# SwiGLU pairs on one Trainium2 core: eleven more pairs by seven products, two kinds of PSUM tile, another order at the seams, the last two output tiles in halves

## The chip, the core and the metric

The kernel runs on one NeuronCore of a Trainium2 chip. The metric is the device time of one execution in microseconds (us). TensorE does the matmuls, VectorE and ScalarE the elementwise work, SyncE issues most of the loads; each engine has its own instruction stream, and semaphores tie them together. Matmul results land in PSUM, everything else is in SBUF.

## What is computed

Two models of depth 2 run one after the other, each on 512 tokens of width 1024. The stages at issue are the four SwiGLU layers of the second model, where 16 learned tokens stand ahead of the 512 (T = 528; the last layer drops them, T = 512):

```python
def swiglu(x, w_gate, w_up, w_down):
    return (jax.nn.silu(x @ w_gate) * (x @ w_up)) @ w_down

for l in range(DEPTH):
    h = h + 0.5 * swiglu(rmsnorm(h, norm_gains[l, 0]), ...)
    h = h + mixer(rmsnorm(h, norm_gains[l, 1]), ...)
    h = h + 0.5 * swiglu(rmsnorm(h, norm_gains[l, 2]), ...)
return rmsnorm(h, final_norm)[:, N_META:]
```

The width D_FF is 2816, so w_gate and w_up have 22 column tiles of 128 each, and w_down has 22 row tiles. All is float32.

## The kernel before, in words

**Products in three parts.** Each float32 operand is split into a high part in the type fp32r and the rest. For weights the high part, whi, is written by ScalarE (L226) and the rest, wlo, by VectorE (L227); activations are split in the same way by `split` (L235, L236). A product is then three matmuls: high by high, low by high, high by low (L241).

**Stages.** `ffn2(l, f)` is one SwiGLU layer; (0,0), (0,1), (1,0) and (1,1) name the four. Between (0,0) and (0,1), and between (1,0) and (1,1), stands a mixer; (1,0) follows (0,1) at once. A seam is the passage from the end of one such stage to the first round of the next.

**Rounds and pairs.** In ffn2 the 22 gate and up tiles of the same column form 22 pairs. They are computed in three rounds, pairs 0 to 7, 8 to 15 and 16 to 21 (`ROUNDS`); behind each round comes its down product, eight output tiles (dn) whose results are scaled (fd) and added to the residual (xt). Two kinds of pair exist. A direct pair (`whole`) is two groups of 48 matmuls at T = 528 (24 of 512 columns at T = 512), one for the gate, one for the up tile. A seven-product pair (`strassen`) gets the same from seven products p1, p2, p6, p5, p7, p4, p3 of 12 matmuls each, of half the width (264 or 256 columns). For that it needs sums of weights (`sum`, four a pair, VectorE L1049) and sums of activations, the forms: `form(k)` makes fu and fv for one of four row tiles k by one ScalarE operation, four short VectorE ones (tu, tv) and two splits (ful, fvl on VectorE). `DIRECT` names the pairs that are direct, its first tuple for (0,1), (1,0) and (1,1), its second for (0,0).

**The sums of a seven-product pair.** p1 makes Y in PSUM, and ScalarE copies it (L1104); p6, p7 and p4 go on adding to Y, each behind a copy of the stand before it. p2 makes X, p5 makes Z, to which p3 adds; VectorE adds X and Z to the copies (L1098). PSUM has three tiles of two banks (kind P) and two tiles of one bank (kind S). Before, Y and Z lie in P and X in S, and a gate or up group takes a P tile.

**The order.** Inside the rounds the order of TensorE's products is computed by `product_order`, which starts a product as soon as its operands are there by its own cost numbers, at most two pairs at a time, and TensorE is held to it. Weight loads and splits run six products ahead (`LEAD`); there are six raw, four sum and eight whi and wlo buffers. On the other engines instructions run in the order in which they stand, and a waiting one holds up those behind it.

**The seams.** Pairs 0 and 1 are direct and run ahead of the first round (`ahead`; in (0,0) pairs 0, 1 and 2, from products made earlier). Their gate and up groups g0, u0, g1 and u1 follow the arrival of the normalized input. `finish`, called for each output tile at the end of the stage before, splits the input and makes a form for k = 4, 5 and 6; the fourth form is made in the `ahead` loop, before pair 0's result is scaled (`mul_r`, L447), multiplied and split (`act`: L1207 on ScalarE, L1208 on VectorE, then fah on ScalarE and fal on VectorE).

**The end.** In (1,1) the last of the eight output tiles is computed in halves of 256 tokens by `ending`: the first half is finished (sum of squares ssq, reciprocal root by ten small VectorE steps, broadcast bc, eight final multiplications L1310 and their stores) before the second.

The change touches `DIRECT`, `finish` (L331), `strassen` (L1089), `product_order` (L1136), the `ahead` loop in `ffn2` and `ending` (L1281). The changed file has one line more near its top, so a line of before stands there a little lower: L227 becomes L228, L447 L448, L1104 L1106, L1207 L1212.

Of the kernel before, what the change touches and what calls it, by code (L numbers as in the profile page):

```python
# [22 lines left out]
NX = 512  # L23
# [30 lines left out]
DIRECT = (0, 1, 5, 12, 18), (3, 12, 18)  # L54
# [7 lines left out]
class Net:  # L62
    def __init__(self, ctx, tc, d):
        nc = self.nc = tc.nc
        self.tc = tc
        self.d = d
        self.n = 0
        self.xp = ctx.enter_context(tc.tile_pool(name="xp", bufs=1))
        self.cp = ctx.enter_context(tc.tile_pool(name="cp", bufs=1))
        self.sp = ctx.enter_context(tc.tile_pool(name="sp", bufs=NSLOT))  # L70
        self.mp = ctx.enter_context(tc.tile_pool(name="mp", bufs=24))
        self.qp = ctx.enter_context(tc.tile_pool(name="qp", bufs=8))
        self.wstack = ctx.enter_context(ExitStack())
# [257 lines left out]
    def finish(self, k, T, g):  # L331
# [4 lines left out]
        if self.forms is not None and NK // 2 <= k < NK - 1:  # L336
# [734 lines left out]
    def whole(self, i, xs, T, rb, act):  # L1071
# [3 lines left out]
        def one(o):  # L1075
            def go(w):
# [12 lines left out]
    def strassen(self, i, xs, T, rb, act):  # L1089
# [16 lines left out]
        def p2(w):  # L1106
            X = self.S("x")[:, :h]
# [3 lines left out]
        def p6(w):  # L1111
# [3 lines left out]
        def p5(w):  # L1115
            Z = ps["Z"] = self.P("z")[:, 0, :h]
            self.prod(Z, w[0], f1, a, True)

        def p7(w):
# [4 lines left out]
        def p4(w):  # L1124
# [3 lines left out]
        def p3(w):  # L1128
# [7 lines left out]
    def product_order(kinds):  # L1136


        LAT = 24
        need = {"p6": ("p1",), "p5": ("p1",), "p7": ("p6", "p5"), "p4": ("p7",), "p3": ("p7",), "p2": ("p1",)}  # L1140
        takes, frees = {"p1", "p5", "g", "u"}, {"p4", "p3", "g", "u"}
        left = [(m, o) for m, kd in enumerate(kinds) for o in (("p1", "p2", "p6", "p5", "p7", "p4", "p3") if kd == "7" else ("g", "u"))]
        end, out, t = {}, [], 0
        hold = []
        while left:
            first = left[0][0]
            best = None
            for m, o in left:
                if m > first + 1:
                    break  # L1150
                at = max([t] + [end[m, d] + (0 if (d, o) in (("p1", "p2"), ("p1", "p5"), ("p5", "p7")) else LAT) for d in need.get(o, ()) if (m, d) in end])
                if any((m, d) not in end for d in need.get(o, ())):
                    continue
                if o in takes:
                    busy = [f for f in hold if f is None or f > t]
                    if len(busy) >= 3:
                        if None in busy and sum(f is None for f in busy) >= 3:
                            continue
                        at = max(at, sorted(f for f in busy if f is not None)[len(busy) - 3])
                if best is None or at < best[0]:  # L1160
                    best = (at, m, o)
            at, m, o = best
# [3 lines left out]
            if o in takes:  # L1166
                hold = [f for f in hold if f is None or f > at]
                hold.append(t + LAT if o in ("g", "u") else None)
            elif o in frees:
                hold.remove(None)  # L1170
                hold.append(t + LAT)
            out.append((m, o))
        return out

    def ffn2(self, l, f, xs, g, next_g, out=None):
# [45 lines left out]
        for m1 in ROUNDS:  # L1221
# [24 lines left out]
            for n in range(len(order) + LEAD):  # L1246
                if n < len(order):
                    i, o = order[n]
# [3 lines left out]
                if n >= LEAD:  # L1252
                    i, o = order[n - LEAD]
# [4 lines left out]
                    do[i][o](w.pop((i, o)))  # L1258
# [16 lines left out]
            if fin and out is not None:  # L1275
                self.ending(out, self.wload(dsrc(NK - 1)), acts, rb)
# [4 lines left out]
    def ending(self, out, ws, acts, rf):  # L1281

        nc = self.nc
        ps = [self.outs(1, NX, "dn")[0][0] for _ in range(2)]
        m = NK - 1
        for hf in range(2):
            c = slice(256 * hf, 256 * hf + 256)
            bl = (2 * hf, 2 * hf + 1)
            n = len(acts)
            for k in range(n):  # L1290
                self.mm3(ps[hf], ws, 128 * k, acts[k], NX, k == 0, k == n - 1, halves=(hf,))
            xv = self.xt[m][:, c]
            t = self.slot("fd")
            nc.vector.scalar_tensor_tensor(
                out=t[:, c], in0=ps[hf][:, c], scalar=0.5, in1=rf[:, c], op0=ALU.mult, op1=ALU.mult
            )
            nc.vector.tensor_tensor(out=xv, in0=t[:, c], in1=xv, op=ALU.add)
            self.sumsq(m, xv, c)
# [4 lines left out]
            self.finals(out, bc, c)  # L1303
# [758 lines left out]
```

## Time and profile before

| what | value |
|---|---|
| median of 3 runs | 3576.71 us (3575.93 to 3577.52) |
| profiled execution, its own time | 3577.7 us |
| its span | 3575.9 us |
| granted TensorE clock, mean | 0.991 of full |
| TensorE busy | 3501.3 us |
| VectorE busy | 2437.5 us |
| ScalarE busy | 1718.5 us |

The span runs from the first to the last instruction; the profiled execution's own time holds 1.8 us more. Busy times of different engines overlap. The granted clock is what the chip gave TensorE: 1.00 stands for 2.4 GHz, 0.50 for 1.2 GHz.

### The profile page before, as it was taken

How to read it: one execution, taken by the hardware profiler on the slowest of the kernel's cores; microseconds unless marked ns; L12 is line 12 of the kernel's file. 1: busy time of each engine (PE TensorE's matmuls, PEld its weight loads, DVE VectorE, ACT ScalarE, POOL GpSimd, SP SyncE). 2: the span in 40 equal slices, each digit the busy share in tenths (PEclk: the TensorE clock that was granted, in tenths of full speed). 3: DMA queues.
4: the chain of work that ended last, by engine and by line, in shares of the span. 5: the costliest groups of instructions: out<-in, count | busy, mean ns of one | idle time of the engine just before them, and what ended most of it. 6: DMA issues, size and time to landing. Idle time of an engine off the chain costs nothing.

```text
span 3575.9 us, 59662 instructions
## 1 busy us (share of the span) xinstructions
PE 3501.3 (98%) x23291; PEld 3123.4 (87%) x23291; DVE 2437.5 (68%) x4715; ACT 1718.5 (48%) x3151; POOL 44.3 (1%) x184
## 2 busy tenths in 40 slices
PE   8999999999999999999999999999999999999998
PEld 6778888778888899998898999998999987788987
DVE  6778753776874387676545777678677764677767
ACT  3654432365543364354574454454444457545443
POOL 1000000000000000000000000000000000000000
PEclk9999999999999999999999999999999999999999
DMA  4213323212333232331111222332333212223232
GB/s 151 65 48 109 97 89 107 81 60 67 99 95 93 70 105 89 95 107 61 55 61 57 83 92 92 94 102 77 96 107 93 76 54 64 65 85 105 92 104 71
DMA packets 142954, 304.94 MB, mean 85 GB/s; under 512 B 16436, under 2 KB 24660, under 8 KB 142672
## 3 DMA queue, kind: packets, MB, share of 16 engines
q1 hardware_dynamic: 138672, 292.88, 26.1%
q0 software_dynamic: 2560, 6.93, 0.6%
q8 instruction: 183, 3.00, 0.3%
q10 hardware_dynamic: 1440, 1.32, 0.1%
q14 instruction: 99, 0.81, 0.1%
HBM read 298.97 MB, written 2.10 MB: 84 GB/s over the span
## 4 chain that ended last, share of the span: by engine, by line
PE 73%; DVE 5%; ACT 2%; issue 1%; DMA 0%; DVEq 0%; ACTq 0%
PE dn L241 15%; PE g L241 12%; PE y L241 11%; PE up L241 7%; PE gu L241 6%; PE z L241 5%; PE wo L241 3%; PE x L241 3%; PE pa L241 1%; PE pb L241 1%; PE oa L1531 1%; PE sc L1497 1%; DVE wlo L227 1%; PE go L1761 1%; PE ptr L1514 1%
## 5 line engine op out<-in xcount | busy, mean ns | idle before, releaser
L226 ACT ACTIVATE whi<-raw 128x512 fp32r<-128x512 f32 (+3 forms) x880 | 620.0, 708 | 879.2 <-PE dn L241 340.5
L227 DVE TENSOR_TENSOR wlo<-raw,whi 128x512 fp32r<-128x512 f32 (+3 forms) x880 | 687.8, 783 | 401.2 <-ACT whi L226 386.9
L241 PE MATMUL g<-xh,whi 128*128 128x256 f32 (+4 forms) x1192 | 330.4, 333 | 10.0 <-ACT xh L315 5.7
L241 PE MATMUL g<-xl,whi 128*128 128x256 f32 (+4 forms) x1192 | 317.9, 320 | 0.1
L241 PE MATMUL g<-xh,wlo 128*128 128x256 f32 (+4 forms) x1192 | 316.1, 320 | 0.0
L241 PE MATMUL up<-xl,whi 128*128 128x512 f32 (+1 forms) x768 | 288.7, 376 | 0.1
L241 PE MATMUL up<-xh,wlo 128*128 128x512 f32 (+1 forms) x768 | 288.6, 376 | 0.0
L241 PE MATMUL up<-xh,whi 128*128 128x512 f32 (+1 forms) x768 | 287.9, 376 | 0.0
L241 PE MATMUL dn<-fah,whi 128*128 128x256 f32 (+1 forms) x1238 | 286.4, 300 | 1.2 <-ACT fah L235 0.6
L241 PE MATMUL dn<-fah,wlo 128*128 128x256 f32 (+1 forms) x1238 | 285.3, 299 | 0.0
L241 PE MATMUL dn<-fal,whi 128*128 128x256 f32 (+1 forms) x1238 | 285.1, 299 | 0.0
L226 ACT ACTIVATE whi<-sum 128x512 fp32r<-128x512 f32 x268 | 169.2, 632 | 219.0 <-PE dn L241 72.4
L241 PEld LDWEIGHTS g<-xh,whi 128*128 128x128 f32 (+1 forms) x1192 | 198.0, 188 | 46.1 <-issue 18.1
L227 DVE TENSOR_TENSOR wlo<-sum,whi 128x512 fp32r<-128x512 f32 x268 | 184.2, 687 | 47.9 <-ACT whi L226 43.7
L241 PEld LDWEIGHTS g<-xh,wlo 128*128 128x128 f32 (+1 forms) x1192 | 200.3, 188 | 15.4
L241 PEld LDWEIGHTS g<-xl,whi 128*128 128x128 f32 (+1 forms) x1192 | 200.7, 189 | 14.1 <-issue 1.6
L241 PEld LDWEIGHTS dn<-fah,whi 128*128 128x128 f32 x1238 | 199.8, 188 | 10.8 <-ACT fah L235 3.9
L241 PEld LDWEIGHTS dn<-fal,whi 128*128 128x128 f32 x1238 | 199.4, 188 | 7.9 <-DVE fal L236 0.8
L241 PEld LDWEIGHTS dn<-fah,wlo 128*128 128x128 f32 x1238 | 199.7, 188 | 7.3
L241 PEld LDWEIGHTS up<-xl,whi 128*128 128x128 f32 x768 | 145.1, 189 | 28.3 <-DVE xl L316 0.5
L241 PEld LDWEIGHTS up<-xh,wlo 128*128 128x128 f32 x768 | 145.2, 189 | 28.0
L241 PEld LDWEIGHTS up<-xh,whi 128*128 128x128 f32 x768 | 144.7, 189 | 27.5
(503 smaller groups left out, 8704.0 us busy)
## 6 DMA issues: line engine op xcount, KB each, us to landing
raw<-w_up SPq DMA_DIRECT2D x88, 512.0 KB, 3.6
raw<-ffn_g SPq DMA_DIRECT2D x176, 256.0 KB, 2.6
raw<-ffn_u SPq DMA_DIRECT2D x176, 256.0 KB, 2.9
raw<-ffn_d SPq DMA_DIRECT2D x160, 256.0 KB, 2.7
raw<-w_in SPq DMA_DIRECT2D x136, 256.0 KB, 2.6
raw<-w_down SPq DMA_DIRECT2D x32, 512.0 KB, 3.5
raw<-w_in SPq DMA_DIRECT2D x25, 512.0 KB, 3.6
raw<-w_out SPq DMA_DIRECT2D x16, 512.0 KB, 3.5
```

The lines of the kernel that those rows point to most:

```text
L226: h = self.nc.scalar.activation(hi[:, c], raw[:, c], AF.Copy)
L227: l = self.nc.vector.tensor_tensor(out=lo[:, c], in0=raw[:, c], in1=hi[:, c], op=ALU.subtract)
L241: i = self.nc.tensor.matmul(*a, **k)
L1497: nc.tensor.matmul(o, lhsT=q, rhs=kk[:, kc], start=i == 0, stop=i == len(ops) - 1)
L1514: nc.tensor.transpose(tr[:, 128 * b : 128 * b + 128], p[:, 128 * b : 128 * b + 128], self.ident)
L1531: nc.tensor.matmul(o[a], lhsT=lh, rhs=rh, start=b == 0, stop=b == 4)
L1761: nc.tensor.matmul(o(b), lhsT=lh, rhs=rh, start=i == 0, stop=i == len(terms) - 1)
```

## The change

Four things are done together.

1. `DIRECT` loses pairs 5, 12 and 18 in (0,1), (1,0) and (1,1), and 12 and 18 in (0,0): by the tuples eleven direct pairs fewer, eight of them at T = 528.
2. `product_order` keeps a model of both kinds of PSUM tile and returns a kind with each product that opens one; `strassen` takes the tile from that kind. p1 prefers P, p2 and p5 prefer S.
3. At the end of the first ffn2 `early` falls from 3 to 2 and stays there, so that `finish` makes two forms ahead of each later seam. In the `ahead` loop pair 0's scaling, and in these three stages its activation too, now stand ahead of the call that makes forms.
4. `ending` works on the last two output tiles: the first half of both, their sum of squares, then the second half of both, the last of these in an S tile (dl). The broadcast is copied to SBUF by ScalarE, and all sixteen final multiplications stand behind the second reciprocal root.

```diff
-DIRECT = (0, 1, 5, 12, 18), (3, 12, 18)
+DIRECT = (0, 1), (3,)
...
+        self.early = 3
...
-        if self.forms is not None and NK // 2 <= k < NK - 1:
+        if self.forms is not None and NK // 2 <= k < NK // 2 + self.early:
             self.form(k - NK // 2, T, g)
...
+        bank = lambda kd, n: self.P(n)[:, 0, :h] if kd == "P" else self.S(n)[:, :h]
...
-        def p1(w):
-            Y = ps["Y"] = self.P("y")[:, 0, :h]
+        def p1(w, kd):
+            Y = ps["Y"] = bank(kd, "y")
...
-            X = self.S("x")[:, :h]
+            X = bank(kd, "x")
...
-            Z = ps["Z"] = self.P("z")[:, 0, :h]
+            Z = ps["Z"] = bank(kd, "z")
...
-        takes, frees = {"p1", "p5", "g", "u"}, {"p4", "p3", "g", "u"}
+        takes = {"p1": "PS", "p5": "SP", "p2": "SP", "g": "P", "u": "P"}
+        frees = {"p4": "p1", "p3": "p5", "p2": "p2", "g": "g", "u": "u"}
...
+        pool, has = {"P": [0] * 3, "S": [0] * 2}, {}
...
+                    at, _, kd = min((max(at, min(pool[q])), j, q) for j, q in enumerate(takes[o]))
...
+                gt = ps[0] if o == 4 else self.mul_r(ps[0], rb, "fg")
+                if not done:
+                    act(o // 2, gt, ps[1], False)
                 forms(1 + (o == 0) - (o == 4))
-                gt = ps[0] if o == 4 else self.mul_r(ps[0], rb, "fg")
-                act(o // 2, gt, ps[1], False)
+                if done:
+                    act(o // 2, gt, ps[1], False)
...
-                self.forms = self.next_forms
+                self.forms, self.early = self.next_forms, 2
...
-            for i in range(NK - 1 if fin and out is not None else NK):
+            for i in range(NK - 2 if fin and out is not None else NK):
...
-                self.ending(out, self.wload(dsrc(NK - 1)), acts, rb)
+                self.ending(out, [self.wload(dsrc(i)) for i in (NK - 2, NK - 1)], acts, rb)
...
-        ps = [self.outs(1, NX, "dn")[0][0] for _ in range(2)]
+        ps = [[self.outs(1, NX, "dn")[0][0] for _ in ws], [self.outs(1, NX, "dn")[0][0], self.S("dl")]]
...
-            self.finals(out, bc, c)
+            rb = self.slot("rbe")
+            nc.scalar.copy(rb[:, c], bc[:, c])
+            bcs.append((rb, c))
+        for rb, c in bcs:
+            self.finals(out, rb, c)
```

What the tables and the code order do to the engines' streams is shown at three places. VectorE at the seam of (0,1), before. Here fal closes pair 0, the row L447 scales pair 1's gate, L1208 multiplies it; ful and fvl are the fourth form's low parts, L1049 the sums of weights:

```order
L236 TENSOR_TENSOR ful_20693<-tu_20685,fuh_20692 128x528
L236 TENSOR_TENSOR fvl_20697<-tv_20686,fvh_20696 128x528
L447 TENSOR_TENSOR fg_20700<-gu_20469,rbc_20620 128x528
L227 TENSOR_TENSOR wlo_20800<-sum_20801,whi_20799 128x512
L227 TENSOR_TENSOR wlo_20806<-raw_20807,whi_20805 128x512
L1208 TENSOR_TENSOR fg_20700<-fg_20700,gu_20470 128x528
L227 TENSOR_TENSOR wlo_20812<-raw_20813,whi_20811 128x512
L236 TENSOR_TENSOR fal_20705<-fg_20700,fah_20704 128x528
L447 TENSOR_TENSOR fg_20769<-gu_20471,rbc_20620 128x528
```

VectorE at the same place, changed; between pair 0's fal and pair 1's scaling (L448) stand twenty rows, four of wlo, four of sum, eight short ones (tu, tv) and four of ful and fvl, of which these are the last eleven:

```order
L228 TENSOR_TENSOR wlo_20917<-raw_20827,whi_20916 128x512
L349 SCALAR_TENSOR_TENSOR tu_20727<-xt_79,v_74,tt_20726 128x264
L1050 TENSOR_TENSOR sum_21033<-raw_20847,sum_20881 128x512
L349 SCALAR_TENSOR_TENSOR tv_20728<-xt_83,v_74,tu_20727 128x264
L355 TENSOR_TENSOR tu_20727<-tv_20728,tt_20726 128x264
L349 SCALAR_TENSOR_TENSOR tv_20728<-xt_83,v_74,tv_20728 128x264
L237 TENSOR_TENSOR ful_20735<-tu_20727,fuh_20734 128x528
L1050 TENSOR_TENSOR sum_21056<-raw_21052,raw_21054 128x512
L237 TENSOR_TENSOR fvl_20739<-tv_20728,fvh_20738 128x528
L448 TENSOR_TENSOR fg_20803<-gu_20489,rbc_20638 128x528
L228 TENSOR_TENSOR wlo_20934<-sum_20935,whi_20933 128x512
```

Pair 0's scaling has moved ahead of the fourth form, and the third and fourth forms have moved between pair 0 and pair 1.

ScalarE at the seam of (0,1), before; L1207 is pair 1's silu, fah its split, COPY the copy of p1's Y:

```order
L226 ACTIVATE whi_20817<-sum_20819 128x512
L1207 ACTIVATE fg_20769<-fg_20769 128x528
L226 ACTIVATE whi_20839<-sum_20847 128x512
L235 ACTIVATE fah_20773<-fg_20769 128x528
L226 ACTIVATE whi_20865<-raw_20793 128x512
L1104 COPY fg_20823<-y_20825 128x264
```

And changed:

```order
L227 ACTIVATE whi_20916<-raw_20827 128x512
L352 ACTIVATE tt_20726<-xt_79,v_74 128x264
L236 ACTIVATE fuh_20734<-tu_20727 128x528
L236 ACTIVATE fvh_20738<-tv_20728 128x528
L227 ACTIVATE whi_20933<-sum_20935 128x512
L1212 ACTIVATE fg_20803<-fg_20803 128x528
L236 ACTIVATE fah_20807<-fg_20803 128x528
L1106 COPY fg_20857<-y_20859 128x264
```

The copy of p1 stands behind pair 1's silu and split as before, and these now stand behind the fourth form's splits.

TensorE at the end of the program, before; ssq is the sum of squares, bc the broadcast, dn_37976 the second half of the last tile:

```order
L241 MATMUL dn_37976<-fal_37702,whi_37970 128x256
L241 MATMUL dn_37976<-fah_37701,wlo_37971 128x256
L365 MATMUL ssq_38001<-cst,acc_37739 128x1 x2
L418 MATMUL bc_38004<-cst,rs_y_38007 128x128 x2
L365 MATMUL ssq_38069<-cst,acc_37739 128x1 x2
L418 MATMUL bc_38072<-cst,rs_y_38075 128x128 x2
```

And changed:

```order
L242 MATMUL dn_38283<-fah_38032,whi_38264 128x256
L366 MATMUL ssq_38333<-cst,acc_38070 128x1 x2
L242 MATMUL dn_38283<-fal_38033,whi_38264 128x256
L242 MATMUL dn_38283<-fah_38032,wlo_38265 128x256
L419 MATMUL bc_38336<-cst,rs_y_38339 128x128 x2
L242 MATMUL dl_38284<-fah_37421,whi_38270 128x256
```

All of the last tile's second half (dl, 18 matmuls) now follows the first broadcast.

## Rows read from the trace of the kernel before

**Rows 1.** The page, part 1: busy us, share of the span, instructions of each engine.

```profile
PE 3501.3 (98%) x23291; PEld 3123.4 (87%) x23291; DVE 2437.5 (68%) x4715; ACT 1718.5 (48%) x3151; POOL 44.3 (1%) x184
```

**Rows 2.** Windows with no other filter: four seven-product pairs of stage (0,1); window, length, busy.

```profile
2188.80:2226.90 38.10, 38.10 (x316) 38.10 (x315) 32.64 (x56) 23.10 (x46) 0.00 (x0) 1.00 0.38 121
```

**Rows 3.** PE timeline of stage (0,1), T=528: start us, us, engine, line, operation, tiles.

```profile
2103.56 0.40 PE L241 MATMUL gu<-xh,whi 128*128 128x256 f32 x2
...
2109.37 0.28 PE L241 MATMUL y<-fuh,whi 128*128 128x264 f32 x1
...
2119.55 0.29 PE L241 MATMUL y<-xh,whi 128*128 128x264 f32 x1
...
2121.01 0.28 PE L241 MATMUL x<-xh,whi 128*128 128x264 f32 x1
```

**Rows 4.** PE timeline of stage (1,1), T=512: a direct group, and the product after it.

```profile
3254.58 0.39 PE L241 MATMUL gu<-xh,whi 128*128 128x512 f32 x1
...
3260.12 0.28 PE L241 MATMUL y<-fuh,whi 128*128 128x256 f32 x1
```

**Rows 5.** Lines by form, DVE, 2180 to 2280 us: count, busy us, mean ns, idle before.

```profile
L227 DVE TENSOR_TENSOR wlo<-sum,whi 128x512 fp32r<-128x512 f32 x26 | 17.9, 688 | 5.0 <-ACT whi L226 4.5
```

**Rows 6.** PE timeline: first and last of three waits of p6 (y); idle before in brackets.

```profile
2125.23 0.39 PE L241 MATMUL y<-fvh,whi 128*128 128x264 f32 x1 [1.14 <-ACT fg L1104]
...
3275.57 0.39 PE L241 MATMUL y<-fvh,whi 128*128 128x256 f32 x1 [1.23 <-ACT fg L1104]
```

**Rows 7.** DVE timeline at the seam of (0,1): fal, pair 1's scaling, its product.

```profile
2074.70 0.71 DVE L236 TENSOR_TENSOR fal<-fg,fah 128x528 fp32r<-128x528 f32 x1
2075.32 0.70 DVE L447 TENSOR_TENSOR fg<-gu,rbc 128x528 f32<-128x528 f32 x1
...
2077.99 0.70 DVE L1208 TENSOR_TENSOR fg<-fg,gu 128x528 f32<-128x528 f32 x1
```

**Rows 8.** ACT timeline at the seam of (0,1): the copy of p1.

```profile
2079.79 0.36 ACT L1104 COPY fg<-y 128x264 f32<-128x264 f32 x1
```

**Rows 9.** PE timeline at the seam of (0,1): first matmuls of p5 (z) and p6 (y).

```profile
2080.17 0.28 PE L241 MATMUL z<-fuh,whi 128*128 128x264 f32 x1
...
2081.62 0.28 PE L241 MATMUL y<-fvh,whi 128*128 128x264 f32 x1
```

**Rows 10.** DVE timeline at the seam of (1,0): a form's short step, the next row.

```profile
2439.91 0.48 DVE L348 SCALAR_TENSOR_TENSOR tu<-xt,v,tt 128x264 f32<-128x264 f32 x1
2440.34 0.69 DVE L227 TENSOR_TENSOR wlo<-sum,whi 128x512 fp32r<-128x512 f32 x1
```

**Rows 11.** Timeline at the seam of (1,1): DVE, ACT and PE, the same places.

```profile
3228.11 0.68 DVE L447 TENSOR_TENSOR fg<-gu,rbc 128x512 f32<-128x512 f32 x1
...
3231.61 0.35 ACT L1104 COPY fg<-y 128x256 f32<-128x256 f32 x1
...
3231.86 0.28 PE L241 MATMUL z<-fuh,whi 128*128 128x256 f32 x1
...
3233.27 0.28 PE L241 MATMUL y<-fvh,whi 128*128 128x256 f32 x1
```

**Rows 12.** PE timeline at the seam of (1,0): u1's first matmul, the next product.

```profile
2445.99 0.78 PE L241 MATMUL gu<-xh,whi 128*128 128x256 f32 x2 [4.37 <-DVE fg L447]
...
2454.10 0.28 PE L241 MATMUL y<-xh,whi 128*128 128x264 f32 x1
```

**Rows 13.** Windows, seam of (1,0), columns as in Rows 2; PEclk: granted clock.

```profile
2441.60:2446.00 4.40, 0.03 (x2) 0.04 (x1) 4.40 (x9) 1.79 (x4) 0.00 (x0) 0.77 0.00 0
2446.00:2448.00 2.00, 2.00 (x9) 2.00 (x10) 1.18 (x3) 1.16 (x2) 0.00 (x0) 0.50 0.19 52
```

**Rows 14.** The chain of waits that ended last, from 3555 us: start us, us, what.

```profile
3556.95 0.62 PE ssq L365 x4
...
3560.34 3.22 DVE fy L1310 x8
...
3568.51 1.21 PE bc L418 x4
```

More of the change, by code (lines that the diff above doesn't have):

```diff
@@ L1075, in one, with go @@
         def one(o):
-            def go(w):
+            def go(w, kd):
                 p = self.outs(1, T, "gu")[0]
@@ L1122, in p7, with p4, p3 @@
             tt(u[:, b], ps["Z"], u[:, b], ALU.add)
-        def p4(w):
+        def p4(w, kd):
             self.prod(ps["Y"], w[0], f2, b, False)
             nc.scalar.copy(u[:, a], ps["Y"])
-        def p3(w):
+        def p3(w, kd):
             self.prod(ps["Z"], w[0], x2, b, False)
@@ L1140, in product_order @@
         need = {"p6": ("p1",), "p5": ("p1",), "p7": ("p6", "p5"), "p4": ("p7",), "p3": ("p7",), "p2": ("p1",)}
-        takes, frees = {"p1", "p5", "g", "u"}, {"p4", "p3", "g", "u"}
+        takes = {"p1": "PS", "p5": "SP", "p2": "SP", "g": "P", "u": "P"}
+        frees = {"p4": "p1", "p3": "p5", "p2": "p2", "g": "g", "u": "u"}
         left = [(m, o) for m, kd in enumerate(kinds) for o in (("p1", "p2", "p6", "p5", "p7", "p4", "p3") if kd == "7" else ("g", "u"))]
         end, out, t = {}, [], 0
-        hold = []
+        pool, has = {"P": [0] * 3, "S": [0] * 2}, {}
+        inf = 10**9
         while left:
@@ L1150, in product_order @@
                     break
-                at = max([t] + [end[m, d] + (0 if (d, o) in (("p1", "p2"), ("p1", "p5"), ("p5", "p7")) else LAT) for d in need.get(o, ()) if (m, d) in end])
                 if any((m, d) not in end for d in need.get(o, ())):
                     continue
+                at = max([t] + [end[m, d] + (0 if (d, o) in (("p1", "p2"), ("p1", "p5"), ("p5", "p7")) else LAT) for d in need.get(o, ())])
+                kd = None
                 if o in takes:
[L1155 to L1159, printed above, removed]
+                    at, _, kd = min((max(at, min(pool[q])), j, q) for j, q in enumerate(takes[o]))
+                    if at >= inf:
+                        continue
                 if best is None or at < best[0]:
-                    best = (at, m, o)
-            at, m, o = best
+                    best = (at, m, o, kd)
+            at, m, o, kd = best
             t = at + (48 if o in ("g", "u") else 12)
@@ L1165, in product_order @@
             left.remove((m, o))
[L1166 to L1172, printed above, removed]
+            if kd:
+                j = pool[kd].index(min(pool[kd]))
+                pool[kd][j] = inf
+                has[m, o] = kd, j
+            if o in frees:
+                q, j = has[m, frees[o]]
+                pool[q][j] = t + LAT
+            out.append((m, o, kd))
         return out
@@ L1247, in ffn2 @@
                 if n < len(order):
-                    i, o = order[n]
+                    i, o, _ = order[n]
                     if i not in get:
@@ L1252, in ffn2 @@
                 if n >= LEAD:
-                    i, o = order[n - LEAD]
+                    i, o, kd = order[n - LEAD]
                     m = ms[i]
@@ L1257, in ffn2 @@
                         do[i] = f(m - m0, xs, T, rb, act)
-                    do[i][o](w.pop((i, o)))
+                    do[i][o](w.pop((i, o)), kd)
             self.pinned = False
@@ L1283, in ending @@
         nc = self.nc
-        ps = [self.outs(1, NX, "dn")[0][0] for _ in range(2)]
-        m = NK - 1
+        ps = [[self.outs(1, NX, "dn")[0][0] for _ in ws], [self.outs(1, NX, "dn")[0][0], self.S("dl")]]
+        n = len(acts)
+        bcs = []
         for hf in range(2):
@@ L1288, in ending @@
             bl = (2 * hf, 2 * hf + 1)
[L1289 to L1298, printed above, removed]
+            for m, p, w in zip((NK - 2, NK - 1), ps[hf], ws):
+                for k in range(n):
+                    self.mm3(p, w, 128 * k, acts[k], NX, k == 0, k == n - 1, halves=(hf,))
+                xv = self.xt[m][:, c]
+                t = self.slot("fd")
+                nc.vector.scalar_tensor_tensor(
+                    out=t[:, c], in0=p[:, c], scalar=0.5, in1=rf[:, c], op0=ALU.mult, op1=ALU.mult
+                )
+                nc.vector.tensor_tensor(out=xv, in0=t[:, c], in1=xv, op=ALU.add)
+                self.sumsq(m, xv, c)
             pss = self.S("ssq")
```

8 lines of the change are left out of this document (4 added, 4 removed).

## The prediction

> **What bounds the kernel now.** The page's first part comes first: TensorE is busy for 98% of the span, VectorE for 68%, ScalarE for 48% [rows 1]. So the time is TensorE's time, and an edit pays by taking matmuls out, or costs by making TensorE stand. The share of 68% is a mean over stages, so the windows come second: in four seven-product pairs of stage (0,1) TensorE has no gap in 38.10 us, and VectorE works 32.64 us of them, 86% [rows 2]. Third, the timelines of TensorE, VectorE and ScalarE at the places that the change touches: the first round of each stage, the seams between stages, and the end.
>
> **The pairs.** By the two tuples the change turns eleven direct pairs into seven-product pairs (its words say ten): eight at T=528 and three at T=512. At T=528 one group of 48 matmuls takes 2109.37 - 2103.56 = 5.81 us, so a direct pair 11.62; one product takes 2121.01 - 2119.55 = 1.46, so seven take 10.22 [rows 3]. That saves 1.40 us, times eight 11.2. At T=512 a group takes 3260.12 - 3254.58 = 5.54 [rows 4], a pair 11.08; a product 3233.27 - 3231.86 = 1.41 [rows 11], seven 9.87; that saves 1.21, times three 3.6. Together **-14.8 us**, all of it on the path. Each new pair also asks for more of VectorE: three more weight subtractions and four weight sums, some 0.69 us each [rows 5], and three additions. That is costed at nothing: the four pairs in a row of [rows 2] are made of such pairs alone, and VectorE still has 14% to spare. If that cover were gone, the saving would go with it (a rival below). DMA issues do not grow.
>
> **Waits that go.** In the first round of (0,1), (1,0) and (1,1), p6 of the pair that follows a direct pair stands 1.1 to 1.2 us for ScalarE's copy of p1, which is queued behind the direct pair's activation [rows 6] (the first and the last of the three; the middle one took 1.13). No direct pair stands there any more, so these go: 1.14 + 1.13 + 1.23 = **-3.5 us**. In (0,0) a direct pair stays in front, and I take nothing.
>
> **PSUM kinds.** In the new order p2 and p5 take the one-bank kind S, p1 the two-bank kind P. In [rows 2] TensorE does not wait for a P tile, so a third free P tile earns nothing: 0. The cost side is a rival.
>
> **The seams of (0,1) and (1,1).** This is the term that decides. Two of the four operand forms, not one, are now left for the seam, and VectorE's order puts both behind pair 0's last subtraction (fal) and ahead of pair 1's scaling. Before, the scaling followed that fal at once, 2074.70 to 2075.32 [rows 7]. Now twenty rows stand between: four weight subtractions, four weight sums and four splits at the 0.62 us step of [rows 7], and eight short steps of forms at 2440.34 - 2439.91 = 0.43 [rows 10]. That is 12 x 0.62 + 8 x 0.43 = 10.9 us: the scaling comes at 2086.2. Two things wait. p5 needs the fourth form's first half, ready some 1.2 us before that, at 2085.0, where it began at 2080.17 [rows 9]. And p6 needs the copy of p1, which in ScalarE's order stands behind pair 1's activation and split, so behind that scaling: from scaling to copy it took 2079.79 - 2075.32 = 4.47 us [rows 7, 8]; one row fewer stands on VectorE between scaling and product now, so 3.85, and 0.36 for the copy itself. p6 then starts at 2090.4 instead of 2081.62 [rows 9]: **+8.8 us**. In (1,1) the same rows have a step of 0.60, the short ones 0.41 (estimates by the sizes, 512 to 528): 10.5 us later, scaling at 3238.6; copy 3231.61 - 3228.11 = 3.50 later, 0.35 long; p6 at 3242.5 instead of 3233.27 [rows 11]: **+9.2 us**.
>
> **The clock after them.** At the seam of (1,0) TensorE stood 4.37 us [rows 12], and in the window after it the granted clock was 0.50, the lower of the two levels (1.2 against 2.4 GHz) [rows 13]. The group that followed took 2454.10 - 2445.99 = 8.11 us instead of 5.81 [rows 12, 3]: 2.3 more. The new stalls are longer, 5 and 4 us with one product between, so each gets that price: **+4.6 us**, between 0 (the clock holds) and 4.6. The Trainium skill, "TensorE: Matmul & The Clock Gate", Part 1, says that an idle TensorE is throttled to half rate and must work for a while before it is let up again; [rows 13] agree, and by the page's rule alone the sum would hold the same 4.6.
>
> **The seam of (1,0).** Here the fourth form stood ahead of pair 0's scaling and held the 4.37 us wait. With the scaling first, that wait goes (up to 4.37 + 2.3 = 6.7 gained). But VectorE works without a break there, 4.40 us of 4.40 [rows 13], and the same rows still have to pass before p6: the wait moves from u1 to p5 and p6. I take **0**, since the row shows VectorE as the bound; ends -6.7 and +2.3 (a second half-clock stretch).
>
> **The end.** Two tiles in halves: the first sum of squares can start one half-tile group earlier (18 matmuls at half of 5.54/24 us, 2.1) and no longer behind a whole tile's addition (an estimate: 0.5): -2.6. The first eight finals, 3.22 us [rows 14], move from the middle to the end: 0, but they hide the second broadcast there (-1.2 [rows 14]). The last half tile's 18 matmuls now come behind the first broadcast: +2.1, or 4.2 at half clock. **-1.7 us**, ends -2.6 and +0.4.
>
> **Sum.** -14.8 - 3.5 - 1.7 + 8.8 + 9.2 + 4.6 + 0 = +2.6 us. The profiled execution took 3577.7 us, 1.0 above the median of the runs shown; against the median 3576.7 the sum gives **3579.3 us**: no difference that a measurement here tells (0.2% is 7.2 us, about what it can tell).
>
> **Rivals.**
> *Short seams (faster).* Only the moved third form comes on top (4 x 0.43 + 2 x 0.62 = 3.0 us a seam), because the weight rows among the twenty run in the time in which VectorE would wait anyway, and the clock holds. Then 8.8 + 9.2 + 4.6 = 22.6 becomes about 6: 3563. For it: over the whole span VectorE is idle for a third of the time [rows 1]. Against it: none of the rows of VectorE at this place shows an idle time ahead of it [rows 7]. Chance 0.17.
> *Longer seams (slower).* The weight subtractions among the twenty need buffers that only TensorE frees, and TensorE stands. Each of the two seams then loses some 3 to 4 us more: five or six more of the 0.62 us steps [rows 7], 3579.3 + 6 to 9 = 3585 to 3588. It decides when a subtraction of the twenty waits over 1 us for TensorE. Chance 0.13.
> *S as the bound (slower).* X and Z share two tiles; p2 or p5 waits until VectorE has added the Z before it. It decides once that addition comes later than two products, 2.9 us, after its product. At 0.2 us a pair and 78 pairs it costs 15.6: 3595. [rows 2] speak against it: VectorE keeps up. Chance 0.08.
> *VectorE as the bound (slower), or the pairs bring nothing.* With no direct pair to catch up in, the missing 14% is used up and the 14.8 is not earned: 3594. Against it: [rows 2]. Chance 0.05.
> *The clock in the rounds (slower).* TensorE halves in every round because tiles are handed over more often: twelve rounds at 2.3 us, 3607. The granted clock of [rows 2] is 1.00. Chance 0.02. The Trainium skill, "TensorE: Matmul & The Clock Gate", "A second HAM failure mode: psum-queue depth-cycling", tells of a kernel that cycles its PSUM banks and whose clock swings with the short idles between; no row here shows that.
> That leaves 0.55 for the forecast, whose own range is 3574 to 3585.
>
> **Numbers.** Range 3567 to 3589: it leaves out the lower half of the short seams and the last three rivals, about 0.2. Faster by over 0.2% (below 3569.6): 0.16, the short seams almost whole. Slower (above 3583.9): the three last rivals 0.15, most of the longer seams and the top of the forecast's range, 0.26 together. Within: 0.58.
>
> **What would show it.** Right: TensorE gaps of 4 to 5 us in front of p5 and p6 at 2080 to 2090 and around 3240 on the shifted scale, released by VectorE's ful and ScalarE's copy, clock 0.50 behind them; no gaps before p6 in the first rounds; a round of eight sevens without gaps; 78 copies of p1. Wrong: seams below 4 us in all, a wait of p2 on the addition of Z, or VectorE over 97% in the rounds.

## The result: slower, by waits in every round

The changed kernel takes 3598.2 us (median of 4 runs, 3596.8 to 3600.4), the kernel before beside it 3577.05 us; the ratio is 1.0060, 95% interval 1.0045 to 1.0074. Forecast were 3579.3 us and a range of 3567 to 3589: the time is above the range. Its profiled execution took 3598.57 us, span 3596.8 us, against 3577.7 and 3575.9.

The page of the changed kernel, its first line, the busy times (part 1) and one of the costliest groups (part 5; behind the second bar the idle time of TensorE just before the group, and what ended most of it):

```profile
span 3596.8 us, 59926 instructions
PE 3495.2 (97%) x23321; PEld 3121.7 (87%) x23321; DVE 2481.3 (69%) x4828; ACT 1749.1 (49%) x3231; POOL 44.4 (1%) x184
L242 PE MATMUL y<-fvh,whi 128*128 128x264 f32 (+1 forms) x624 | 181.9, 291 | 29.7 <-ACT fu L1123 18.0
```

TensorE is busy for 6.1 us less than before [rows 1], where 14.8 was worked out for the pairs, and its idle time grew from 74.6 to 101.6 us, so the span grew by 20.9 us: TensorE stands more. The third line tells where. The matmuls y<-fvh belong to p6 and p4; before them stand 29.7 us of idle time, and 18.0 of these end with ScalarE's copy L1123, that of p7. Most of the rest, 11.5 us, are waits of p6 at the seams for the copy of p1. Before, the same group by shape, T = 528, had 3.4 us of idle time in all, put down to the copy of p1 [rows 6], and none to that of p7:

```profile
L241 PE MATMUL y<-fvh,whi 128*128 128x264 f32 x400 | 115.1, 288 | 3.4 <-ACT fg L1104 3.4
```

The windows of the second round of (0,1), before, then changed, whole, and of the 9.3 us behind its longest wait, columns as in [rows 2]:

```profile
2188.80:2273.50 84.70, 84.68 (x695) 84.31 (x694) 70.14 (x117) 49.15 (x95) 0.00 (x0) 1.00 0.36 113
2196.30:2284.40 88.10, 85.72 (x688) 85.15 (x687) 73.75 (x127) 51.48 (x102) 0.00 (x0) 0.98 0.34 108
2218.70:2228.00 9.30, 9.29 (x64) 9.29 (x65) 6.70 (x13) 4.55 (x10) 0.00 (x0) 0.82 0.35 114
```

This round took 84.7 us before, with no gap. TensorE was to gain 1.4 us in it; it has no matmul for 2.4 us, and the mean granted clock of the whole round is 0.98, since it falls to 0.82 behind the wait. VectorE works 73.75 of 88.10 us, 84%: it is not at its limit.

What makes the wait, in that round. VectorE's timeline, then ScalarE's, then TensorE's:

```profile
2215.17 0.68 DVE L228 TENSOR_TENSOR wlo<-sum,whi 128x512 fp32r<-128x512 f32 x1
2215.88 0.69 DVE L1050 TENSOR_TENSOR sum<-raw,sum 128x512 f32<-128x512 f32 x1
2216.49 0.70 DVE L1213 TENSOR_TENSOR fg<-fg,fu 128x528 f32<-128x528 f32 x1
```

```profile
2217.23 0.64 ACT L236 ACTIVATE fah<-fg 128x528 fp32r<-128x528 f32 x1 [0.78 <-DVE fg L1213]
2217.78 0.61 ACT L227 ACTIVATE whi<-sum 128x512 fp32r<-128x512 f32 x1
2218.30 0.36 ACT L1123 COPY fu<-y 128x264 f32<-128x264 f32 x1
```

```profile
2218.71 0.39 PE L242 MATMUL y<-fvh,whi 128*128 128x264 f32 x1 [1.76 <-ACT fu L1123]
```

Product p7 of the second pair began at 2212.40 and takes 1.46 us, so it had ended by 2213.9, and ScalarE needs 0.36 us for the copy, yet the copy starts at 2218.30. ScalarE takes its instructions in order, and ahead of the copy stand the split of the first pair's activation (fah), which waits for VectorE's product L1213 at 2216.49, and a weight split. That product in turn stands on VectorE behind a weight subtraction and a weight sum. p4, the product that adds to the copied Y, starts 0.4 us behind the copy, 1.76 us late. Such a wait of p4 stands once in each of the twelve rounds, 1.25 to 1.76 us long, 16.9 us together, and twice a second one, 0.50 and 0.62: the 18.0 us of the page.

Why there. In the old order the second pair begins p1 p2 p6, then come the first pair's p4 and p3, then the second pair's p5 and p7. Z had to wait for a P tile. In the new order Z takes an S tile, so p5 goes ahead of the first pair's p4 and p3, and the first pair's activation comes one product, 1.46 us, later against the second pair's p7 and p4. Between the end of the first pair's p3 and the second pair's p4 TensorE then has three products to do, 4.4 us, and no longer four, while the activation and the copy queued behind it took 6.3 us from the end of p3. One product was about all the slack there was.

The seam of (0,1), changed, to be read beside [rows 7 to 9]: VectorE, ScalarE, TensorE, and the windows with the granted clock in the third column from the right:

```profile
2072.57 0.71 DVE L237 TENSOR_TENSOR fal<-fg,fah 128x528 fp32r<-128x528 f32 x1
...
2082.27 0.71 DVE L237 TENSOR_TENSOR ful<-tu,fuh 128x528 fp32r<-128x528 f32 x1 [0.30 <-ACT fuh L236]
...
2084.12 0.70 DVE L448 TENSOR_TENSOR fg<-gu,rbc 128x528 f32<-128x528 f32 x1
```

```profile
2086.79 0.64 ACT L236 ACTIVATE fah<-fg 128x528 fp32r<-128x528 f32 x1 [1.30 <-DVE fg L1213]
2087.34 0.36 ACT L1106 COPY fg<-y 128x264 f32<-128x264 f32 x1
```

```profile
2082.29 0.39 PE L242 MATMUL z<-fuh,whi 128*128 128x264 f32 x1 [2.96 <-ACT fuh L236]
...
2087.75 0.59 PE L242 MATMUL y<-fvh,whi 128*128 128x264 f32 x1 [4.09 <-ACT fg L1106]
```

```profile
2084.00:2088.00 4.00, 0.25 (x1) 0.25 (x2) 3.26 (x6) 1.72 (x4) 0.00 (x0) 0.50 0.00 0
2088.00:2090.00 2.00, 2.00 (x10) 2.00 (x11) 0.51 (x2) 0.00 (x0) 0.00 (x0) 0.50 0.00 0
```

Pair 1's scaling comes 11.55 us behind fal, where the prediction had 0.62 + 10.9; the copy of p1 3.2 us behind it. p6 waits for that copy as described; p5's first matmul is released by ScalarE's fuh, and ful holds it back by 0.35 us more. The first matmul of p1, before, then changed:

```profile
2077.24 0.28 PE L241 MATMUL y<-xh,whi 128*128 128x264 f32 x1
```

```profile
2075.15 0.28 PE L242 MATMUL y<-xh,whi 128*128 128x264 f32 x1
```

From it to the first matmul of p6 it is 2087.75 - 2075.15 = 12.60 us, and was 2081.62 - 2077.24 = 4.38 [rows 9]: +8.2. In (1,1) it is 12.62 and was 4.28: +8.3. Behind the stalls p6 and the two products after it took 7.1 and 6.1 us instead of 4.4 and 4.3, the clock's part: +4.5 in the two seams.

The end, in the chain of waits (start, duration, what), beside [rows 14]:

```profile
3575.80 0.62 PE ssq L366 x4
3578.43 1.22 PE bc L419 x4
3579.66 3.12 PE dl L242 x18
3587.22 1.98 DVE fy L1324 x5
```

The 18 matmuls of dl take 3.12 us, with a mean granted clock of 0.67 in that stretch. From the first matmul of the last two tiles to the end of the span it was 27.9 us before and is 27.5 now.

### The profile page after: what moved, and what is told of

Same layout as the page of the kernel before. It is cut to its first block, busy times and chain, and to the rows that moved or that the text cites. A ratio compares the mean times of both kernels' runs of the same rounds, so it can differ in the third digit from the quotient of the medians.

```text
span 3596.8 us, 59926 instructions
## 1 busy us (share of the span) xinstructions
PE 3495.2 (97%) x23321; PEld 3121.7 (87%) x23321; DVE 2481.3 (69%) x4828; ACT 1749.1 (49%) x3231; POOL 44.4 (1%) x184
## 3 DMA queue, kind: packets, MB, share of 16 engines
q10 hardware_dynamic: 1440, 1.32, 0.1%
## 5 line engine op out<-in xcount | busy, mean ns | idle before, releaser
L228 DVE TENSOR_TENSOR wlo<-raw,whi 128x512 fp32r<-128x512 f32 (+3 forms) x869 | 680.0, 784 | 388.3 <-ACT whi L227 376.3
L227 ACT ACTIVATE whi<-sum 128x512 fp32r<-128x512 f32 x312 | 197.0, 631 | 237.3 <-PE y L242 83.5
L228 DVE TENSOR_TENSOR wlo<-sum,whi 128x512 fp32r<-128x512 f32 x312 | 213.7, 686 | 65.5 <-ACT whi L227 63.0
L242 PE MATMUL y<-fvh,whi 128*128 128x264 f32 (+1 forms) x624 | 181.9, 291 | 29.7 <-ACT fu L1123 18.0
L242 PE MATMUL y<-fvh,wlo 128*128 128x264 f32 (+1 forms) x624 | 179.2, 287 | 0.0
L242 PE MATMUL y<-fvl,whi 128*128 128x264 f32 (+1 forms) x624 | 179.0, 287 | 0.0
```

The source lines that it names most:

```text
L227: h = self.nc.scalar.activation(hi[:, c], raw[:, c], AF.Copy)
L228: l = self.nc.vector.tensor_tensor(out=lo[:, c], in0=raw[:, c], in1=hi[:, c], op=ALU.subtract)
L242: i = self.nc.tensor.matmul(*a, **k)
```

## The experiments

Two theories stood against each other after the first reading. By *order*, the new order of products brings p4 one product nearer to the activation behind which its copy is queued, and costs that in every round whatever VectorE has to do. By *load*, VectorE is late because eleven pairs more are formed by products.

**Old order in the changed kernel.** `product_order` and the kinds of tile are those of before, all else is as changed:

```diff
-        takes = {"p1": "PS", "p5": "SP", "p2": "SP", "g": "P", "u": "P"}
-        frees = {"p4": "p1", "p3": "p5", "p2": "p2", "g": "g", "u": "u"}
+        takes, frees = {"p1", "p5", "g", "u"}, {"p4", "p3", "g", "u"}
...
+            out.append((m, o, {"p1": "P", "p5": "P", "p2": "S"}.get(o)))
```

> The changed kernel with the product order and the PSUM kinds of before (Y and Z in P, X in S); pairs, seams and ending as changed. Theory 'order': the new order brings p5 of the second pair ahead of the first pair's p4 and p3, so the first pair's activation comes one product (1.46 us) later, ScalarE's copy of the second pair's p7 (L1123) stands behind that activation's split, and the second pair's p4 waits 1.3 to 1.8 us, once in every round. With the old order these 12 waits go, with the half-clock stretches behind the longer ones: 18 to 24 us less than the changed kernel's 3598, so 3574 to 3580, and no gap over 0.5 us in the second and third rounds. Rival 'load': the waits come from VectorE, which has more weight rows to do with eleven direct pairs fewer; they stay whatever the order, 3595 to 3600.

Measured: 3574.97 us (10 runs, 3573.2 to 3576.7), 23.2 less than the changed kernel; ratio to before 0.9995 (0.9985 to 1.0004). The second round of (0,1) in its windows, and the y<-fvh groups by shape:

```profile
2189.40:2273.70 84.30, 83.90 (x687) 83.55 (x687) 73.77 (x127) 51.52 (x102) 0.00 (x0) 1.00 0.36 113
```

```profile
L242 PE MATMUL y<-fvh,whi 128*128 128x264 f32 x464 | 134.3, 290 | 2.1 <-ACT fu L1123 2.0
L242 PE MATMUL y<-fvh,whi 128*128 128x256 f32 x160 | 46.0, 288 | 0.4 <-ACT fu L1123 0.4
```

VectorE's work in the round is the same to 0.02 us, 73.77, and the waits have shrunk from 18.0 to 2.4 us. So the load alone does not make them; it takes the order. One wait of 1.34 us is left in the second round of (0,0), where no gap over 0.5 was expected. The waits are 15.6 of the 23.2 us; the rest was not taken apart. Order and kinds were changed back together, but no wait for an S tile shows in the changed kernel either: the idle time in front of p2's first matmuls (x<-xh) is 0.0. ScalarE and TensorE at the place of the wait, with the old order:

```profile
2208.03 0.65 ACT L236 ACTIVATE fah<-fg 128x528 fp32r<-128x528 f32 x1 [0.35 <-DVE fg L1210]
2208.58 0.61 ACT L227 ACTIVATE whi<-raw 128x512 fp32r<-128x512 f32 x1
2209.10 0.36 ACT L1123 COPY fu<-y 128x264 f32<-128x264 f32 x1
```

```profile
2209.83 0.28 PE L242 MATMUL y<-fvh,whi 128*128 128x264 f32 x1
```

The copy stands behind fah here too. It ends 0.4 us ahead of p4, which now comes four products behind the first pair's p3 and waits for nothing. The seam of (0,1) has one wait instead of two, in front of p5:

```profile
2081.09 0.56 PE L242 MATMUL z<-fuh,whi 128*128 128x264 f32 x1 [7.13 <-DVE fg L448]
```

Z then has to have the P tile that pair 1's scaling frees, so all of the stall stands there.

**Old seams in the changed kernel.**

```diff
+                forms(1 + (o == 0) - (o == 4))
                 gt = ps[0] if o == 4 else self.mul_r(ps[0], rb, "fg")
-                if not done:
-                    act(o // 2, gt, ps[1], False)
-                forms(1 + (o == 0) - (o == 4))
-                if done:
-                    act(o // 2, gt, ps[1], False)
+                act(o // 2, gt, ps[1], False)
...
-                self.forms, self.early = self.next_forms, 2
+                self.forms, self.early = self.next_forms, 3
```

> The changed kernel with the seams of before (three forms made by finish, forms ahead of pair 0's scaling); pairs, order and ending as changed. Theory 'order': seams and rounds add up; the two seams gave 8 to 9 us each and some 2.5 us of half clock, so this is 19 to 22 us faster than the changed kernel, 3576 to 3579, and the waits of p4 in the rounds stay as they are. Rival 'seam taken up later': the work on VectorE is the same, and what does not wait at the seam waits in the first round; under 8 us faster, over 3590.

Measured: 3583.57 us (10 runs, 3579.2 to 3589.0), 14.6 less than the changed kernel, where 19 to 22 were expected: a miss, between the two theories. The stalls of (0,1) and (1,1) are gone, that of u1 at the seam of (1,0), 4.38 us, is back, and part is taken up in the same round: the first wait of p4 in (0,1), 1.26 us in the changed kernel, is now

```profile
2103.21 0.39 PE L242 MATMUL y<-fvh,whi 128*128 128x264 f32 x1 [2.35 <-ACT fu L1123]
```

and that of (1,1) 2.77 instead of 1.37. That VectorE catches up behind a stall, and that without it the activation is later, would explain this; it was not tested. Its runs also spread over 10 us, more than those of most others here.

**New order and kinds alone, in the kernel before.** The edit is the diff's part on `strassen` and `product_order`.

> The kernel before with the new product order and PSUM kinds alone; direct pairs, seams and ending as before. Theory 'order': the wait of p4 appears where a round begins with three seven-product pairs, in the first round of three stages and in the second of all four, 7 waits of 1.4 to 1.9 us, some with half clock: 3587 to 3593, against 3577 of before. Rival 'load': nothing changes, since the load is that of before: 3575 to 3579. Rival 'two S tiles': more waits than these seven, released by VectorE's additions L1099, over 3593.

Measured: 3588.82 us (5 runs, 3587.1 to 3590.0), ratio 1.0035 (1.0022 to 1.0048). With before's direct pairs the new order alone costs 11.9 us. ScalarE and TensorE in the second round of (0,1):

```profile
2211.68 0.64 ACT L235 ACTIVATE fah<-fg 128x528 fp32r<-128x528 f32 x1 [0.65 <-DVE fg L1212]
2212.23 0.61 ACT L226 ACTIVATE whi<-sum 128x512 fp32r<-128x512 f32 x1
2212.75 0.36 ACT L1122 COPY fu<-y 128x264 f32<-128x264 f32 x1
```

```profile
2213.16 0.39 PE L241 MATMUL y<-fvh,whi 128*128 128x264 f32 x1 [1.26 <-ACT fu L1122]
```

The same three rows stand in the same order as in the changed kernel. Such waits of p4, 1.26 to 1.35 us long, stood in five rounds, not in the seven expected: in the first rounds of three stages, behind the direct pairs, there are none. The five come to 6.5 us, the larger part of the 11.9; the five rounds that hold them are longer by 1.7 to 1.9 us each than in the kernel before, 8.9 of the 10.9 us between the two profiles. Load alone is refuted a second time: here it was that of before.

**New table of direct pairs alone.**

```diff
-DIRECT = (0, 1, 5, 12, 18), (3, 12, 18)
+DIRECT = (0, 1), (3,)
```

> The kernel before with the new table of direct pairs alone; order by the old rules, seams and ending as before. Theory 'order': the eleven pairs bring what was worked out, 14.8 us, and the three waits of p6 go, 3.5 us: 3557 to 3561. Rival 'load': VectorE has no direct pair to catch up in, the waits of 1.4 us stand in every round, 3574 to 3580.

Measured: 3559.43 us (4 runs, 3558.7 to 3564.1), ratio 0.9952 (0.9935 to 0.9969): 17.5 us less, where the terms on the pairs and on the waits of p6 came to 18.3. Yet with the old order and the new table p4 waits in six places, 0.29 to 1.32 us and 4.4 us in all, where it waited nowhere before; whether VectorE's greater load or the sequence without direct pairs does that was not separated:

```profile
L241 PE MATMUL y<-fvh,whi 128*128 128x264 f32 x464 | 134.1, 289 | 5.6 <-ACT fu L1121 4.4 <-ACT fg L1104 1.1
```

**The new seams alone, in the kernel before** (the diff's lines on `early`, `finish` and the `ahead` loop):

> The kernel before with the change at the seams alone (two forms by finish, pair 0's scaling and activation ahead of the forms); direct pairs, order, kinds and ending as before. Theory 'seam': two forms behind pair 0 hold pair 1's scaling back by some 10 us in (0,1) and (1,1), and p5 or p6 with it; with the old order p5 waits instead of p6, since its P tile is freed by that scaling. 3589 to 3594 against 3577 of before. Rival 'seam taken up later': under 5 us, 3577 to 3582.

Measured: 3594.03 us (4 runs, 3590.8 to 3596.8), ratio 1.0048 (1.0034 to 1.0061), 17.3 us more. TensorE in front of p5 at the seam of (0,1):

```profile
2084.30 0.56 PE L242 MATMUL z<-fuh,whi 128*128 128x264 f32 x1 [7.33 <-DVE fg L448]
```

The wait is ended by pair 1's scaling, as in the changed kernel with the old order.

**The new ending alone:**

> The kernel before with the new ending alone. The prediction's term was -1.7 us: 3574.5 to 3576. Theory from the changed kernel's trace: the two first halves' additions stand behind those of the whole tile before them on VectorE (a chain of 3.4 us), and the last half tile runs at half clock behind the wait for the first broadcast, 3.1 us for 18 matmuls, so the ending is 0.5 to 1 us longer: 3577.3 to 3578.3.

Measured: 3576.26 us (11 runs, 3575.0 to 3579.9) against 3576.72; ratio 1.0000 (0.9991 to 1.0008). Neither a gain of 1.7 us nor a loss of 1 can be told from this: inconclusive.

**The copy ahead of the activation.** The changed kernel with the old seams, in whose rounds each pair's activation is issued one product later, behind the second pair's p7:

```diff
-            act(i, s, u[:, :T], True)
+            self.late.append(lambda: act(i, s, u[:, :T], True))
...
+                    go, self.late = self.late, []
                     do[i][o](w.pop((i, o)), kd)
+                    for f in go:
+                        f()
...
```

> The changed kernel with the seams of before, and in the rounds each pair's activation is issued one product later, so that ScalarE's copy of the next pair's p7 stands ahead of the activation's split; the new order and kinds stay. Theory 'order' (the copy's place in ScalarE's queue is what p4 waits for): the waits of 1.3 to 2.8 us in all twelve rounds go, 18 to 24 us less than the 3583.6 of the same kernel without it: 3559 to 3566. Rival: p4 waits for something else (VectorE's load, the S tiles), the time stays within 4 us of 3583.

Measured: 3565.08 us (6 runs, 3562.3 to 3568.4), 18.5 less than without the edit. Order, kinds and work are the same; each pair's activation stands one product later on ScalarE and on VectorE, so that the copy is ahead of it on ScalarE. The waits of p4 have shrunk from 20.1 us to 6.4. Where one product later is not enough for the copy, a wait stays, nine in all, 0.27 to 1.08 us long, as in the third round of (0,0):

```profile
1553.94 0.39 PE L243 MATMUL y<-fvh,whi 128*128 128x264 f32 x1 [0.84 <-ACT fu L1124]
```

**Pair 0's scaling ahead of the fourth form, with the new table.**

```diff
-                forms(1 + (o == 0) - (o == 4))
                 gt = ps[0] if o == 4 else self.mul_r(ps[0], rb, "fg")
+                forms(1 + (o == 0) - (o == 4))
                 act(o // 2, gt, ps[1], False)
```

> The kernel before with the new table of direct pairs, and at the seams pair 0's scaling ahead of the fourth form, its activation behind it; finish still makes three forms. Theory: at the seam of (1,0) the fourth form held back the scaling that frees the P tile of u1's group; that wait of 4.4 us and the half clock behind it (2.3 us) go, and one form behind the scaling is short enough not to be seen: 4 to 7 us less than the 3559.4 with the table alone, 3552 to 3556. Rival: VectorE works without a break there and is the bound, so the wait only moves to p5 and p6: 3558 to 3561.

Measured: 3556.86 us (4 runs, 3553.8 to 3558.8), ratio 0.9943 (0.9930 to 0.9957), 2.6 less than with the table alone; against the 4 to 7 expected that is short, and the two sets of runs overlap. VectorE at the seam of (1,0), and the window of 18.7 us in which TensorE stood 4.4 us before [rows 12, 13]:

```profile
2432.70 0.71 DVE L447 TENSOR_TENSOR fg<-gu,rbc 128x528 f32<-128x528 f32 x1 [0.28 <-PE gu L241]
...
2436.69 0.70 DVE L236 TENSOR_TENSOR ful<-tu,fuh 128x528 fp32r<-128x528 f32 x1
```

```profile
2431.30:2450.00 18.70, 18.70 (x155) 18.67 (x155) 17.36 (x30) 11.54 (x23) 0.00 (x0) 1.00 0.21 64
```

The scaling now stands four microseconds ahead of the fourth form's ful, TensorE has no gap, and the clock stays at 1.00. The form itself makes p5 no later: VectorE was not the bound here, the order on it was.

**All of what helped, with either order.** The new table, pair 0's scaling first, and each activation three products later:

```diff
-            act(i, s, u[:, :T], True)
+            self.late.append((2, lambda: act(i, s, u[:, :T], True)))
...
+                    self.late = [(n - 1, f) for n, f in self.late]
+                    go = [f for n, f in self.late if n < 0]
+                    self.late = [x for x in self.late if x[0] >= 0]
...
```

with the order, kinds and ending of before:

> The kernel before with the new table of direct pairs, pair 0's scaling ahead of the fourth form at the seams, and in the rounds each pair's activation issued three products later, so that it stands behind the copy of the next pair's p7 on ScalarE in every place of the order. Theory 'order': the small waits of p4 that are left without it (0.3 to 0.9 us, seven of them) go: 2 to 5 us less than 3556.9, 3552 to 3555. Rival: the later activation holds tiles longer and is late for the down product, 3557 or more.

Measured: 3553.81 us (5 runs, 3548.6 to 3554.5), ratio 0.9933 (0.9921 to 0.9946). And with the new order, kinds and ending:

> The same with the new product order and PSUM kinds and the new ending: Z in an S tile, p5 earlier. Theory: once the copy does not stand behind the activation, the kinds earn and cost nothing, since no product waits for a PSUM tile in either order: within 3 us of the run beside it, 3551 to 3556. Rival 'two S tiles': p2 waits for the addition of Z (L1099) and it is slower by over 4 us.

Measured: 3546.51 us (5 runs, 3544.1 to 3550.6), ratio 0.9918 (0.9905 to 0.9932): the fastest of all, 30.6 us less than before. ScalarE at the place of the wait, and the y<-fvh groups by shape:

```profile
2196.96 0.36 ACT L1124 COPY fu<-y 128x264 f32<-128x264 f32 x1
2197.98 0.65 ACT L1213 ACTIVATE fg<-fg 128x528 f32<-128x528 f32 x1 [0.65 <-DVE fg L1212]
...
2199.53 0.65 ACT L237 ACTIVATE fah<-fg 128x528 fp32r<-128x528 f32 x1
```

```profile
L243 PE MATMUL y<-fvh,whi 128*128 128x264 f32 x464 | 133.2, 287 | 0.0
L243 PE MATMUL y<-fvh,whi 128*128 128x256 f32 x160 | 45.2, 282 | 0.9 <-ACT fg L1107 0.9
```

The copy now stands ahead of the silu and of fah. The group's idle time of 29.7 us, 18.0 in the rounds and 11.5 at the seams, has come down to 0.9, and none of it is put down to p7's copy. The 7.3 us between the two kernels were not expected. In their profiles 2.9 us lie in the first rounds of (0,1), (1,0) and (1,1), where the old order has short waits of p3, p4 and p1, 1.7 behind the start of the last two tiles, and 3.3 in the mixer between (0,0) and (0,1), which no edit touches and where the granted clock differed (see the last section). At the same mean granted clock of 0.992 the runs took 3553.7 to 3554.5 and 3550.4 to 3550.6 us, 3 to 4 us apart. How much of that is the kinds' and how much the ending's was not separated.

**One form behind pair 0 instead of two.** The changed kernel, in which `finish` still makes three forms:

```diff
-                self.forms, self.early = self.next_forms, 2
+                self.forms, self.early = self.next_forms, 3
```

> The changed kernel, but with three forms made by finish, so that one form, not two, stands between pair 0's activation and pair 1's scaling. Theory 'seam': the stall is as long as the rows of VectorE that stand there; with about half the rows some 5 us a seam go and the rest of the stall and the half clock stay in part: 3584 to 3590 between the changed kernel's 3598 and the 3583.6 with the seams of before. Rival: the place of the activation alone makes the stall, 3595 to 3600.

Measured: 3580.68 us (10 runs, 3575.2 to 3584.1), 17.5 less than the changed kernel and below the expected 3584. At the seam of (0,1) the two waits of 2.96 and 4.09 us are one:

```profile
2084.82 0.39 PE L242 MATMUL y<-fvh,whi 128*128 128x264 f32 x1 [2.83 <-ACT fg L1106]
```

So most of the seams' loss was the second form; the place of the activation alone is not what makes the stall.

## Why the prediction was wrong

The sum came to +2.6 us, and +21 was measured. Point by point:

- *The pairs*, -14.8, and *waits that go*, -3.5: right in size. The table alone gave -17.5 us. In the changed kernel the three waits of p6 are gone from the first rounds too. The table alone also brought 4.4 us of waits of p4, which the sum had put at nothing.
- *PSUM kinds: 0.* This is the step that failed. I asked whether a third free P tile earns anything and took the new order of products as free, because neither kind of tile is waited for. I did not follow what the order does to ScalarE's queue, though a wait of just this kind, a copy behind an activation, stood in [rows 6]. The runs show 18.0 us of such waits in the changed kernel, a clock of 0.81 and 0.82 over the 9 us behind two of them, and the same kernel 23.2 us faster with the old order. Alone, in the kernel before, the order cost 11.9; without direct pairs all twelve rounds begin with the sequence that waits, so the parts do not add up: 11.9 - 17.5 + 17.3 - 0.5 gives +11, and the whole is +21. Taken one behind the other they do: -17.5 for the table, then +15.5 for seams and ending (3574.97 with the old order), then +23.2 for the order. Without the order the changed kernel can't be told from the one before, and 3574.97 lies inside the range that was given: the order is what took the time out of it.
- *The seams of (0,1) and (1,1)*, +8.8 and +9.2, and *the clock after them*, +4.6: the mechanism and the places were right. p6 came 8.2 us later in (0,1) and 8.3 in (1,1), with the clock at 0.50 behind the waits and 4.5 us for it. The copy of p1 released p6, as named; what released p5 was ScalarE's fuh and not VectorE's ful. In (1,1) the working left out the row fewer between scaling and product that it took off in (0,1); without that slip it gives 8.6. At their places the three terms are 21.0, where 22.6 was worked out; in the time the seams cost less, 17.3 us alone and 14.6 in the changed kernel, partly because without the stalls other waits grow. The Trainium skill's rule that was weighed there, "TensorE: Matmul & The Clock Gate", Part 1, agrees: 0.50 in the window behind the stalls.
- *The seam of (1,0)*: 0 was right for the changed order, where u1's wait of 4.4 us went and waits of 1.9 and 3.5 us stood before p5 and p6. The reason given was not: VectorE worked without a break, and yet p5 and p6 need not have waited, as the scaling ahead of one form shows.
- *The end*, -1.7: alone it can't be told from 0. The last half tile's matmuls took 3.12 us, midway between the 2.1 and 4.2 given, since the lower clock held for a part of them only.
- *The rivals.* Slower by VectorE's load, by two S tiles or by the clock had 0.15 together. The one that came true was not among them: a copy queued behind an activation on ScalarE. That two S tiles had 3595 and VectorE's load 3594, near the 3598 measured, is chance: p2 waited for no addition, and VectorE worked 84% of the round looked at. Of what would show, I had right that no gaps stand in front of p6 in the first rounds; the gaps at the seams were 3.0 and 3.2 us in front of p5 and 4.1 and 3.9 in front of p6, not 4 to 5. "A round of eight sevens without gaps" was wrong, and it was the line to look at.

## What to carry to other kernels

When an order of products changes, follow each result into the queue of the engine that evacuates it: a copy of 0.36 us cost TensorE 1.3 to 1.8 us each time, because an activation that waits for a third engine stood ahead of it. Issue the short copy that the bound engine needs ahead of the long chain that it does not need yet; with that, the same order that cost 23 us was part of the fastest kernel here. Work that is moved into a hand-over between stages is counted by the rows that then stand ahead of the next release, not by its own length.

## What the runs showed that was not expected

Waits of nearly the same length left different clocks behind them. In the changed kernel 1.76 us and 1.74 us were followed by 0.82 and 0.81 over the next 9 us, and 1.69 us by 1.00; with one form behind pair 0, a wait of 1.78 us was followed by 1.00. The windows behind the waits of 1.74 and 1.69 us, then behind that of 1.78:

```profile
2598.00:2607.00 9.00, 8.93 (x60) 8.93 (x61) 6.36 (x12) 4.33 (x10) 0.00 (x0) 0.81 0.31 107
1312.80:1322.00 9.20, 9.20 (x75) 9.20 (x76) 7.74 (x14) 5.45 (x12) 0.00 (x0) 1.00 0.39 118
```

```profile
2585.60:2594.60 9.00, 9.00 (x74) 9.00 (x75) 7.88 (x15) 5.30 (x12) 0.00 (x0) 1.00 0.35 119
```

From the length of one wait these rows do not tell whether the clock falls.

The clock also moves the time where no edit is. These are the windows of the first mixer of the second model, from the last matmul of the down product before it to the first gate matmul behind it, in the kernel with all of what helped, first with the old order, then with the new:

```profile
1605.40:2045.60 440.20, 429.45 (x3557) 398.89 (x3556) 264.19 (x637) 237.16 (x462) 6.41 (x23) 0.98 0.20 62
1606.50:2043.40 436.90, 426.16 (x3557) 395.54 (x3556) 264.12 (x637) 237.40 (x461) 6.49 (x23) 1.00 0.20 62
```

The same 3557 instructions of TensorE take 3.3 us less at a mean granted clock of 1.00 than at 0.98, and all of it is busy time, 426.16 against 429.45 us. Runs of one kernel differ likewise: those with the old seams took 3579.2 us at a mean clock of 0.992 and 3589.0 at 0.988. So a difference of 3 us between two single profiles says nothing about an edit until the clocks have been compared.
